# Forget gates of all heads made in three steps between Strassen pairs, with one PSUM bank for each product

## The chip, the cores and the metric

The kernel runs on one core of a Trainium2 chip. A core has a matrix engine (TensorE, PE in the rows) with its weight load (PEld), an elementwise engine (VectorE, DVE), an activation engine (ScalarE, ACT), a general one (GpSimd, POOL), and SyncE (SP), which here only issues transfers. Each has its own queue and works it in order; they wait for one another by semaphores. The metric is the time of one execution in microseconds (us), the median of several runs.

## The reference

One decoder block on 512 tokens of width 1024, in float32. The change touches the combined input projection and the gated linear attention (GLA, 4 heads, key width 128, value width 256, chunks of 64 tokens):

```
h = rms_norm(x);  proj = h @ w_in          # q, k, v, r, low-rank a, NSA q/k/v, gates
log_a = log_sigmoid(a_lr @ w_alpha2 + b_alpha) / 16
b = cumsum(log_a) inside each chunk;  b_last = b at the chunk's end
qe, ke, kd = q*exp(b), k*exp(-b), k*exp(b_last - b)
o = causal(qe @ ke^T) @ v + qe @ state;  state = exp(b_last)*state + kd^T @ v
o = rms_norm(o) * silu(r)
x = x + rms_norm((sig(gA)*(o @ w_gla) + sig(gB)*(nsa @ w_nsa)) @ w_out)
x = x + rms_norm(swiglu(rms_norm(x)))
```

## The kernel before

Every float32 operand of the large products is held as a high and a low part, and a product is three matmuls (high by high, high by low, low by high). The program is one stream of instructions for each engine; Python loops write it, and a scheduler fixes the order in each queue when the kernel is built, by its own estimate of when operands are there. `tc.issue_after(x)` puts what is made under it behind instruction x in its engine's order.

**Stages.** Up to 42.5 us of the span, part of the input projection is made token-major (`tok_chunk`). Then come eleven *pairs* of output tiles (loop at L542): each pair is one 2x2 Strassen step on two tiles of 128 columns of `w_in`, with 7 products of 12 matmuls of 256 columns (`in_unit`, L384 to L423). Pairs 0 to 3 are q and k of the four GLA heads (`gq`, `gk`), 4 to 7 the eight tiles of r (`rr`), 8 the selected and window keys (`kst`), 9 and 10 the NSA queries (`qst`). They end at 163.84 us. Then comes linear attention (`gla_prep`, `gla_attn`, `gla_turn`, `gla_state`, `gla_out`, `gla_end` for each head), put by the table `when` (L759) between steps of other matmuls: 16 steps that make the values of heads 2 and 3 (`values_step`) and then eighths of dense products. After 250 us follow sparse attention, projections and the feed-forward part.

**A pair.** The first tile g is loaded into one of three `wraw` buffers, the second tile u into one of two `urw` (L328, issued two pairs ahead by SP; pair 0 has them the other way round). VectorE makes four sums of them (`in_sums`, L355 to L358: s1, s2 in one `ssum` buffer, s3, s4 in the other). Sums and raw tiles are split: ScalarE casts the high part (L221, L336), and the low part is a subtraction on VectorE (L222) or, for raw tiles, a negated copy on ScalarE (L337) and an accumulating transfer on GpSimd's queue (L338). The parts live in five slots used in turn (`s0`, `s1`, `s2`, and two of `whi`/`wlo`); those of a22 in `uu`. In this order the products are: a11 into r1, s2 into r2, s3 into rb, s1 into ra, a22 added to rb, s4 added to ra, a12 added to r1. After the first, ScalarE copies r1 to `us` (L403); VectorE adds r2 to it (`us`, L400), then makes `us` + rb before a22 may be added to rb, and so on; the last part is a copy on ScalarE (L415) and a scaling (L418, L421); r tiles get a Silu on ScalarE (L423).

**Banks.** PSUM has eight banks, two for each of the tags sc, mm, acc and tp. A pair uses both banks of one tag (r1 and rb in halves of the first, r2 and ra in halves of the second), and the tag changes from pair to pair.

**Gates.** `gate_logs` (L427) makes the forget gates of two heads: load the second-layer weights (GpSimd), clear and fill `w3` (VectorE), four transposes of the low-rank columns of `tokb`, copies (`aT`), for each head one gate product (L445) with an Abs on ScalarE (L446) and a min on VectorE (L447), then Exp and Ln on both heads (L449, L450), each function in its own table that ScalarE loads first (ACT_TABLE_LOAD), and for each head a subtraction and a scan along the tokens (L452, L453). It runs in pair 6 for heads 0 and 1 (`early_gates`, tiles `ge`) and in linear attention for heads 2 and 3 (`late_gates`, tiles `gl`, at step 5 of `when`).

**A head of linear attention.** `gla_prep` makes five exponentials on ScalarE (L598 to L604: `e1`, two parts of `e2`, `dd`, and the small `el`; `el`, `dd` and most products have two buffers), `dec` (L606) and four products on VectorE, and four on GpSimd (L616, L620 to L622) that use `el` and `dd`. `gla_attn` has four matmuls and a masked copy into `at` on VectorE (L634), `gla_turn` three transposes and a copy `gkut` on ScalarE, `gla_state` three products (L650), each in its own tp bank (there are two), read by ScalarE (L652) or VectorE, `gla_out` seven products (L666, L668), four squares (L669) and four scaled copies on ScalarE, `gla_end` eight transposes (L682).

## Time and profile before

| | before |
|---|---|
| median of three runs | 872.01 us (871.56, 872.01, 1165.77) |
| the profiled execution | 871.92 us, of which the span of the trace is 870.1 us |
| mean granted clock of TensorE | 0.988 of full speed |
| busy: TensorE / VectorE / ScalarE / GpSimd | 840.0 / 652.2 / 534.8 / 155.7 us |
| stage 0 to 42.5 us | TensorE busy 41.45 of 42.50 us |
| pairs, 42.5 to 163.84 us | TensorE busy 114.90 of 121.34 us, clock 0.97 |
| linear attention, 163.84 to 250 us | TensorE busy 75.70 of 86.16 us, clock 0.96 |
| the rest, 250 to 870 us | TensorE busy 607.92 of 620.00 us, clock 0.99 |

The span runs from the first to the last instruction in the trace; the time of an execution has 1.8 us more. A timeline row gives the start, the length, engine, line, operation, output<-inputs, shapes and count, and in brackets how long the engine had been idle before it and which instruction ended that. Matmuls overlap their neighbours, so their lengths add up to more than the time between starts. Tile names stand without buffer numbers. The clock is given as a share of the full 2.4 GHz.

### The profile page before, as it was taken

The page shows a single profiled execution, that of the slowest core. Times are in us where ns is not written, and L with a number is a line of the kernel's source. Part 1 is how long each engine was busy: PE and PEld are TensorE (multiplying, and loading weights), DVE is VectorE, ACT ScalarE, POOL GpSimd, SP SyncE. Part 2 cuts the span into 40 slices and gives each one's busy share as a digit, 9 for nine tenths or more (in the row PEclk, how much of TensorE's full clock was granted, in tenths as well). Part 3 has the DMA queues.
Part 4 walks back from the last instruction along what each step waited for, and adds up shares of the span by engine and source line. Part 5 has one row for each costly group of instructions (what it writes and reads, how often), then busy time and mean ns, then how long its engine had stood idle before and what let it go on. Part 6 is the DMA issues. An engine that isn't in the chain of part 4 may idle for free.

```text
span 870.1 us, 14830 instructions
## 1 busy us (share of the span) xinstructions
PE 840.0 (97%) x5632; PEld 765.3 (88%) x5632; DVE 652.2 (75%) x1219; ACT 534.8 (61%) x945; POOL 155.7 (18%) x186
## 2 busy tenths in 40 slices
PE   9999989978999999999999999999999999999995
PEld 8999979957788788888887999899999999889995
DVE  7888768755465888887767468998778779838886
ACT  6765666456453788888744576866666557535441
POOL 0121112213030001000000354111111110001353
PEclk9999989989999999999999999999999999999998
DMA  7588755211142434544316849679877872225222
GB/s 258 153 222 189 156 135 125 74 50 47 34 155 66 121 85 114 118 112 107 86 49 218 277 137 250 138 194 226 185 174 189 192 173 76 93 88 169 87 97 98
DMA packets 43463, 119.99 MB, mean 138 GB/s; under 512 B 5772, under 2 KB 11164, under 8 KB 43264
## 3 DMA queue, kind: packets, MB, share of 16 engines
q1 hardware_dynamic: 30576, 82.49, 29.7%
q0 software_dynamic: 12096, 36.01, 22.6%
q8 instruction: 44, 0.72, 0.3%
q10 hardware_dynamic: 720, 0.54, 0.2%
q14 instruction: 27, 0.22, 0.1%
HBM read 104.34 MB, written 4.19 MB: 125 GB/s over the span
## 4 chain that ended last, share of the span: by engine, by line
PE 81%; ACT 5%; DVE 3%; POOL 2%; issue 1%; DMA 1%; DVEq 0%; ACTq 0%; POOLq 0%
PE ps_mm L204 6%; PE ps_mm L206 6%; PE ps_mm L205 6%; PE ps_mm L1425 6%; PE ps_sc L1425 6%; PE ps_tp L1425 6%; PE ps_acc L1425 5%; PE ps_sc L1717 4%; PE ps_mm L396 3%; PE ps_acc L396 3%; PE ps_sc L396 3%; PE ps_acc L1717 2%; PE ps_mm L1717 2%; PE ps_tp L396 2%; PE ps_tp L1026 2%
## 5 line engine op out<-in xcount | busy, mean ns | idle before, releaser
L79 ACT CAST whi<-wraw 128x1024 fp32r<-128x1024 f32 (+3 forms) x58 | 56.2, 970 | 58.9 <-issue 18.0
L204 PE MATMUL ps_mm<-hT_hi,whi 128*128 128x512 f32 x168 | 69.3, 412 | 0.0
L205 PE MATMUL ps_mm<-hT_lo,whi 128*128 128x512 f32 x168 | 66.8, 398 | 0.0
L206 PE MATMUL ps_mm<-hT_hi,wlo 128*128 128x512 f32 x168 | 66.8, 398 | 0.0
L85 DVE TENSOR_TENSOR wlo<-wraw,whi 128x1024 fp32r<-128x1024 f32 (+3 forms) x43 | 46.7, 1087 | 20.6 <-ACT whi L79 20.5
L83 POOL DMA_DIRECT2D wlo<-wraw x15 | 13.0, 864 | 159.9 <-ACT wlo L82 159.9
L986 ACT ACTIVATE p<-p,mx 128x512 f32<-128x512 f32 (+1 forms) x64 | 35.9, 561 | 8.5 <-DVE mx L984 7.8
L222 DVE TENSOR_TENSOR pl<-ps_tp,ph 128x512 fp32r<-128x512 f32 (+1 forms) x64 | 31.0, 489 | 13.4 <-ACT ph L221 12.8
L206 PEld LDWEIGHTS ps_mm<-hT_hi,wlo 128*128 128x128 f32 x168 | 31.6, 188 | 7.6 <-DVE wlo L85 0.3
L204 PEld LDWEIGHTS ps_mm<-hT_hi,whi 128*128 128x128 f32 x168 | 31.7, 188 | 6.4
L205 PEld LDWEIGHTS ps_mm<-hT_lo,whi 128*128 128x128 f32 x168 | 31.7, 189 | 5.3
L984 DVE CUSTOM_DVE_ANT_0 p<-ps_sc,causal 128x512 f32<-128x512 f32 (+1 forms) x64 | 30.2, 485 | 6.0 <-PE ps_sc L977 5.8
L1324 POOL DMA_DIRECT2D w_uu<-in_w_up x19 | 16.4, 865 | 87.2 <-ACT w_uu L1322 20.4
L221 ACT CAST ph<-ps_tp 128x512 fp32r<-128x512 f32 (+1 forms) x64 | 26.3, 415 | 4.6 <-PE ps_tp L1026 3.8
L1026 PE MATMUL ps_tp<-ident,p 128*128 128x128 f32 x160 | 27.7, 273 | 0.4 <-ACT pc L920 0.3
L1026 PEld LDWEIGHTS ps_tp<-ident,p 128*128 128x128 f32 x160 | 20.6, 140 | 7.9 <-ACT pc L920 0.7
L204 PE MATMUL ps_mm<-gla_hi,whi 128*128 128x512 f32 x64 | 26.1, 408 | 0.0
L1340 ACT CAST w_d1h<-s 128x1024 fp32r<-128x1024 f32 x13 | 13.6, 1050 | 20.2 <-issue 12.5
L206 PE MATMUL ps_mm<-gla_hi,wlo 128*128 128x512 f32 x64 | 25.2, 394 | 0.0
L205 PE MATMUL ps_mm<-gla_lo,whi 128*128 128x512 f32 x64 | 25.2, 393 | 0.0
L1340 ACT CAST w_hl<-s 128x1024 fp32r<-128x1024 f32 x12 | 12.6, 1047 | 16.6 <-issue 14.6
L1340 ACT CAST w_d0h<-s 128x1024 fp32r<-128x1024 f32 x13 | 13.6, 1048 | 13.5 <-issue 12.4
(1153 smaller groups left out, 3373.0 us busy)
## 6 DMA issues: line engine op xcount, KB each, us to landing
wraw<-in_w_t SPq DMA_DIRECT2D x29, 512.0 KB, 3.8
wraw<-in_w_gate SPq DMA_DIRECT2D x21, 512.0 KB, 5.8
rw<-in_w_up SPq DMA_DIRECT2D x19, 512.0 KB, 4.2
wlo<-wraw POOLq DMA_DIRECT2D x15, 512.0 KB, 4.5
...
```

What stands on the lines that cost most here:

```text
L79: self.cast = self.nc.scalar.copy(hi[:, :cols], raw[:, :cols])
L85: self.nc.vector.tensor_tensor(out=lo[:, :cols], in0=raw[:, :cols], in1=hi[:, :cols].bitcast(F32), op=OP.subtract)
L204: pe.matmul(ps[:, t], wh[:, c], xh(k)[:, t], start=(k == 0), stop=False)
L205: pe.matmul(ps[:, t], wh[:, c], xl(k)[:, t], start=False, stop=False)
L206: marks.append(pe.matmul(ps[:, t], wl[:, c], xh(k)[:, t], start=False, stop=(k == ktot - 1)))
L222: dve.tensor_tensor(out=lo, in0=src, in1=hi.bitcast(F32), op=OP.subtract)
L396: pe.matmul(o, w[:, c], x_of(b, q, low), start=(first and q == 0 and i == 0), stop=(q == 3 and i == 2), skip_group_check=True)
L986: act.activation(out=o, in_=o, func=AF.Exp, scale=-1.0, bias=mx[:, i:i + 1], accum_out=z[:, i:i + 1])
L1026: pe.transpose(tp[:, i * 128:(i + 1) * 128], p[:, OFF[i] + k * 128:OFF[i] + (k + 1) * 128], ident)
L1340: act.copy(hi, t)
L1425: pe.matmul(o, w[:, c], x[q], start=(first and q == 0 and i == 0), stop=(q == 3 and i == 2), skip_group_check=True)
L1717: pe.matmul(o, w[:, c], x[q], start=(first and q == 0 and i == 0), stop=(q == KH - 1 and i == 2), skip_group_check=True)
```

## The change

- **Banks.** Each product of a pair has a bank of its own: r1, r2, rb, ra lie in four banks, (sc, sc, mm, mm) in even pairs and (acc, acc, tp, tp) in odd ones. There is one `us` tile in place of two.
- **Sums.** s3 and s4 are written over the raw tile u in `urw`; there is one `ssum` buffer. The freed room holds the gates of all four heads (`lam01`, `lam23`).
- **Gates.** `gate_logs` is cut into `gates_low` (weights, transposes, `aT`; in pair 3), `gates_in` (gate products, Abs, min; heads 0, 1 in pair 4, heads 2, 3 in pair 5), `gates_logs` (four Exp, four Ln, in pair 5's turn of the loop) and `gates_sums` (subtractions and scans; heads 0, 1 in pair 6, heads 2, 3 in pair 7). `late_gates` is gone.
- **Silu.** All eight are made together after pair 7 (`silu_r`), followed by one small Exp that loads that table. Table loads on ScalarE fall from 9 to 5 in the program.
- **Pairs.** The NSA queries come before the selected and window keys.
- **Linear attention.** The table `when` is spread anew, and `gla_state` puts its first two products in one bank.
- Two small ones: `ones` is one column that is broadcast, and in pair 0 the split of a22 is made before the sums.

The core of the diff:

```diff
+    lam23 = tokv.tile([128, 2, S], F32, name="lam23")
+    spare = tokv.tile([128, 2, S], F32, tag="lam01", name="spare")
...
-    ssum = [s1.tile([128, 1024], F32, name="ssum%d" % i) for i in range(2)]
+    ssum = [s1.tile([128, 1024], F32, name="ssum"), spare.rearrange("p a t -> p (a t)")]
...
-    pairs += [(T_KV + 2, T_KV + 3), (T_NQ, T_NQ + 1), (T_NQ + 2, T_NQ + 3)]
+    pairs += [(T_NQ, T_NQ + 1), (T_NQ + 2, T_NQ + 3), (T_KV + 2, T_KV + 3)]
...
-        g, u, (a, b) = graw[j], uraw[j], ssum
+        g, u, a = graw[j], uraw[j], ssum[0]
...
-        dve.tensor_tensor(out=b[:, lo], in0=g[:, lo], in1=u[:, lo], op=OP.subtract)
-        dve.tensor_tensor(out=b[:, hi], in0=g[:, hi], in1=a[:, hi], op=OP.subtract)
+        dve.tensor_tensor(out=u[:, lo], in0=g[:, lo], in1=u[:, lo], op=OP.subtract)
+        dve.tensor_tensor(out=u[:, hi], in0=g[:, hi], in1=a[:, hi], op=OP.subtract)
...
-        split(hi, lo, ssum[names[0] == "s3"])
+        split(hi, lo, uraw[j] if names[0] == "s3" else ssum[0])
...
+    def in_banks(j):
+        return (("sc", "mm"), ("acc", "tp"))[j % 2]
+
     def in_unit(j):
-        tag = ("sc", "mm", "acc", "tp")[j % 4]
         d1, d2 = [in_dst(n) for n in pairs[j]]
-        p1, p2 = bank(tag), bank(tag)
-        r1, rb, r2, ra = p1[:, 0:256], p1[:, 256:512], p2[:, 0:256], p2[:, 256:512]
-        us = us2[j % 2]
+        r1, r2, rb, ra = [bank(tag)[:, 0:256] for tag in in_banks(j) for _ in range(2)]
+        us = us2[0]
...
-        product(rb, "s3", "t3", False)
+        product(rb, "s3", "t3", True)
         add(us[:, 1, :], rb, us[:, 0, :])
-        product(ra, "s1", "t1", False)
+        product(ra, "s1", "t1", True)
...
-            if n >= T_R:
-                act.activation(out=t, in_=t, func=AF.Silu)
+
+    def silu_r():
+        with tc.issue_after(gst["act"].ins):
+            for t in [rr[i ^ 1] for i in range(8)]:
+                last = act.activation(out=t, in_=t, func=AF.Silu)
+        with tc.issue_after(last.ins):
+            act.activation(out=warm, in_=mhalf[:, 0:1], func=AF.Exp)
...
+    def gates_low(tag):
+        w_a2, keep = place("ksts", [16, 512], F32), place("kstw", [128, 8, 64], F32)
+        aT, w3 = place("qst0", [80, S], F32R), place("qst1", [80, S], F32R)
...
+        gst.update(a=aT, w=w3, keep=keep, low=[])
+        lam01 = tokv.tile([128, 2, S], F32, tag="lam01", name="lam01")
+        for h in range(HG):
+            lams[h] = (lam01, lam23)[h // 2][:, h % 2, :]
...
+    def gates_in(hs, tag):
+        for h in hs:
             ps = bank(tag)
-            pe.matmul(ps, w3[:, h * 128:(h + 1) * 128], aT, start=True, stop=True)
-            act.activation(out=lam[:, i], in_=ps, func=AF.Abs, bias=b_alpha[:, h:h + 1])
-            dve.tensor_scalar(out=lows[i], in0=ps, scalar1=b_alpha[:, h:h + 1], scalar2=0.0,
-                              op0=OP.add, op1=OP.min)
-        act.activation(out=lam, in_=lam, func=AF.Exp, scale=-1.0)
-        act.activation(out=lam, in_=lam, func=AF.Ln, bias=1.0)
-        for i, h in enumerate(hs):
-            dve.tensor_tensor(out=lam[:, i], in0=lows[i], in1=lam[:, i], op=OP.subtract)
-            dve.tensor_tensor_scan(out=lam[:, i], data0=keep.rearrange("p c t -> p (c t)"), data1=lam[:, i],
+            pe.matmul(ps, gst["w"][:, h * 128:(h + 1) * 128], gst["a"], start=True, stop=True)
+            gst["act"] = act.activation(out=lams[h], in_=ps, func=AF.Abs, bias=b_alpha[:, h:h + 1])
+            low = us2[1] if h == 3 else place(("qst2", "qst3", "ksts")[h], [128, S], F32)
+            dve.tensor_scalar(out=low, in0=ps, scalar1=b_alpha[:, h:h + 1], scalar2=0.0, op0=OP.add, op1=OP.min)
+            gst["low"].append(low)
...
+    def gates_logs():
+        for f, kw in ((AF.Exp, dict(scale=-1.0)), (AF.Ln, dict(bias=1.0))):
+            with tc.issue_after(gst["act"].ins):
+                for h in range(HG):
+                    last = act.activation(out=lams[h], in_=lams[h], func=f, **kw)
+            gst["act"] = last
...
+    def gates_sums(hs):
+        for h in hs:
+            dve.tensor_tensor(out=lams[h], in0=gst["low"][h], in1=lams[h], op=OP.subtract)
+            dve.tensor_tensor_scan(out=lams[h], data0=gst["keep"].rearrange("p c t -> p (c t)"), data1=lams[h],
...
-        if j == 6:
-            in_raw_forms(j + 2)
...
+        with tc.issue_after(after.ins), tc.issue_after(queued["pool"].ins):
+            if j == 3:
+                gates_low("tp")
+            elif j == 4:
+                gates_in((0, 1), "mm")
+            elif j == 5:
+                gates_in((2, 3), "tp")
...
-        if j == 6:
-            with tc.issue_after(after.ins), tc.issue_after(queued["pool"].ins):
-                early_gates()
-        if j + 2 < NP and j != 6:
...
+        if j + 2 < NP:
             in_raw_forms(j + 2)
+        if j == 5:
+            gates_logs()
+        elif j in (6, 7):
+            with tc.issue_after(after.ins):
+                gates_sums(((0, 1), (2, 3))[j - 6])
+        if j == 7:
+            silu_r()
...
+        pss = [bank("tp"), bank("tp")]
         for n in range(3):
-            ps = bank("tp")
-            pe.matmul(ps[:, 0:256], kut[:, n, :], value(h, n), start=True, stop=True)
+            ps = pss[n // 2][:, n % 2 * 256:n % 2 * 256 + 256]
+            pe.matmul(ps, kut[:, n, :], value(h, n), start=True, stop=True)
...
-    for at, f, h in ((0, gla_prep, 1), (3, gla_attn, 0), (5, gla_turn, 0), (6, gla_state, 0), (6, gla_attn, 1),
+    for at, f, h in ((0, gla_prep, 1), (3, gla_attn, 0), (5, gla_turn, 0), (6, gla_state, 0), (7, gla_attn, 1),
                      (8, gla_out, 0), (8, gla_turn, 1), (9, gla_prep, 2), (10, gla_state, 1), (12, gla_end, 0),
-                     (12, gla_out, 1), (13, gla_prep, 3), (15, gla_attn, 2), (16, gla_end, 1), (17, gla_turn, 2),
-                     (20, gla_attn, 3), (21, gla_state, 2), (22, gla_turn, 3), (24, gla_out, 2), (27, gla_state, 3),
-                     (31, gla_end, 2), (31, gla_out, 3), (39, gla_end, 3)):
+                     (13, gla_out, 1), (14, gla_prep, 3), (15, gla_attn, 2), (17, gla_end, 1), (18, gla_turn, 2),
+                     (20, gla_attn, 3), (22, gla_state, 2), (23, gla_turn, 3), (25, gla_out, 2), (28, gla_state, 3),
+                     (32, gla_end, 2), (33, gla_out, 3), (41, gla_end, 3)):
...
-    when.setdefault(5, []).append(gates23)
```

What follows shows how instructions stand in the queues before and after; names are the program's, a number behind a name tells buffers apart. The changed file has its own line numbers: L400, L403, L415 and L221 of before are L404, L407, L419 and L222 there, L446 and L449/L450 are L467 and L476, L598 to L604 are L620 to L626.

On ScalarE, before, the logs of heads 0 and 1 (`lam_1305`) stand behind the copy `us` of pair 7's first product (L403) and the cast of a sum, with a table load ahead of each function:

```order
L403 COPY us_425<-ps_tp 128x256
L221 CAST whi<-ssum_164 128x1024
L446 ACTIVATE lam_1305<-ps_mm,vecs 128x512 x2
L449 ACT_TABLE_LOAD
L449 ACTIVATE lam_1305<-lam_1305 128x1024
L221 CAST s0h<-ssum_165 128x1024
L450 ACT_TABLE_LOAD
L450 ACTIVATE lam_1305<-lam_1305 128x1024
```

After the change the same place is at the end of pair 5 (L419 copies its last product); `lam_978` are heads 0 and 1, `lam_159` heads 2 and 3, and the Abs of heads 0 and 1 were made a pair earlier:

```order
L419 COPY r_140<-ps_acc 128x256
L467 ACTIVATE lam_159<-ps_tp,vecs 128x512 x2
L476 ACTIVATE lam_978<-lam_978 128x512 x2
L476 ACTIVATE lam_159<-lam_159 128x512 x2
L476 ACT_TABLE_LOAD
L476 ACTIVATE lam_978<-lam_978 128x512 x2
L476 ACTIVATE lam_159<-lam_159 128x512 x2
L407 COPY us<-ps_sc 128x256
L222 CAST s0h<-ssum 128x1024
L222 CAST whi<-urw_165 128x1024
```

What moved: two Abs, four Exp, a table load and four Ln now stand ahead of the copy of pair 6's first product (L407), where half of that work stood behind such a copy before.

On ScalarE at the start of linear attention, before, the exponentials of heads 0 and 1 (both from `lam_1305`) are followed by a weight cast (L79) and by the copy `gkut` of head 0 (L642):

```order
L598 ACTIVATE e_1798<-lam_1305 128x512
L601 ACTIVATE e_1799<-dd 128x4x64
L602 ACTIVATE e_1799<-lam_1305 128x4x64
L603 ACTIVATE dd<-dd 128x512
L604 ACTIVATE el<-lam_1305 128x8
L598 ACTIVATE e_1838<-lam_1305 128x512
L601 ACTIVATE e_1839<-dd 128x4x64
L602 ACTIVATE e_1839<-lam_1305 128x4x64
L603 ACTIVATE dd<-dd 128x512
L604 ACTIVATE el<-lam_1305 128x8
L79 CAST whi<-wraw 128x1024
L642 COPY gkut<-ps_tp 128x384
```

After, from the `el` of head 1 (its first row) to `gkut` (L664):

```order
L626 ACTIVATE el<-lam_978 128x8
L624 ACTIVATE e_1882<-lam_978 128x4x64
L626 ACTIVATE el<-lam_159 128x8
L623 ACTIVATE e_1882<-dd 128x4x64
L625 ACTIVATE dd<-dd 128x512
L620 ACTIVATE e_2027<-lam_159 128x512
L624 ACTIVATE e_2028<-lam_159 128x4x64
L626 ACTIVATE el<-lam_159 128x8
L79 CAST whi<-wraw 128x1024
L623 ACTIVATE e_2028<-dd 128x4x64
L625 ACTIVATE dd<-dd 128x512
L664 COPY gkut<-ps_tp 128x384
```

What moved: the small `el` of heads 2 and 3 (from `lam_159`) and the exponentials of head 2 now stand ahead of the cast and of `gkut`; `el` still has two buffers.

On VectorE in pair 2, before, a sum of s3, s4 (L357, L358) is written into the second `ssum` buffer, `ssum_165`, from which L222 makes the low part:

```order
L400 TENSOR_TENSOR gq_149<-ps_acc,us_424 128x256
L222 TENSOR_TENSOR s0l<-ssum_165,s0h 128x1024
L400 TENSOR_TENSOR gq_149<-ps_acc,us_424 128x256
L357 TENSOR_TENSOR ssum_165<-wraw,urw_162 128x512
L400 TENSOR_TENSOR gk_153<-ps_acc,us_424 128x256
L418 SCALAR_TENSOR_TENSOR gq_149<-gq_149,rb_x 128x512
L358 TENSOR_TENSOR ssum_165<-wraw,ssum_164 128x512
L421 TENSOR_TENSOR gk_153<-gk_153,rb_x 128x512
```

After, they are written over u itself (`urw_164`, L360, L361), and the low part of the pair before is made from `urw_165`:

```order
L360 TENSOR_TENSOR urw_164<-wraw,urw_164 128x512
L404 TENSOR_TENSOR gq_149<-ps_mm,us 128x256
L223 TENSOR_TENSOR s0l<-urw_165,s0h 128x1024
L404 TENSOR_TENSOR gq_149<-ps_mm,us 128x256
L361 TENSOR_TENSOR urw_164<-wraw,ssum 128x512
L404 TENSOR_TENSOR gk_153<-ps_mm,us 128x256
L422 SCALAR_TENSOR_TENSOR gq_149<-gq_149,rb_x 128x512
L425 TENSOR_TENSOR gk_153<-gk_153,rb_x 128x512
```

What moved: L360 stands one addition earlier than L357 did, and a `urw` buffer is now read by the split L223, so the load that refills it comes behind that split.

## Rows read from the trace of the kernel before

**Rows 1.** Part 1 of the profile's page: busy time, share of the span and instructions of each engine.

```profile
PE 840.0 (97%) x5632; PEld 765.3 (88%) x5632; DVE 652.2 (75%) x1219; ACT 534.8 (61%) x945; POOL 155.7 (18%) x186
```

**Rows 2.** Windows view, of pair 3 and of linear attention. Columns: stretch, its length, busy time and instructions of TensorE, its weight loads, VectorE, ScalarE, GpSimd, granted clock, share of the DMA engines, GB/s.

```profile
74.22:84.17 9.95, 9.95 (x86) 9.95 (x85) 8.04 (x14) 5.62 (x9) 1.73 (x2) 1.00 0.79 184
...
163.84:250.00 86.16, 75.70 (x354) 60.78 (x353) 49.18 (x81) 49.50 (x112) 26.74 (x38) 0.96 0.20 61
```

**Rows 3.** Timeline of TensorE: ten of its instructions that waited, from 47 to 232 us.

```profile
47.07 0.39 PE L396 MATMUL ps_sc<-tfh,s2h 128*128 128x256 f32 x1 [1.30 <-ACT us L403]
...
97.80 0.38 PE L396 MATMUL ps_mm<-tfh,s2h 128*128 128x256 f32 x1 [0.41 <-ACT us L403]
...
118.93 0.39 PE L396 MATMUL ps_tp<-tfh,whi 128*128 128x256 f32 x1 [0.28 <-ACT us L403]
...
124.07 1.22 PE L445 MATMUL ps_mm<-ge,ge 80*128 80x512 f32 x2 [3.69 <-DVE ge L442]
...
138.32 0.39 PE L396 MATMUL ps_sc<-tfh,whi 128*128 128x256 f32 x1 [0.75 <-DVE us L400]
...
181.14 1.22 PE L445 MATMUL ps_tp<-gl,gl 80*128 80x512 f32 x2 [4.81 <-DVE gl L442]
...
193.86 0.70 PE L666 MATMUL ps_sc<-tok,at 128*128 128x256 f32 x2 [1.70 <-ACT go L669]
...
199.77 0.70 PE L650 MATMUL ps_tp<-tok,gkut 128*128 128x256 f32 x2 [1.16 <-ACT gs L652]
...
215.27 0.66 PE L682 MATMUL ps_tp<-ident,go 128*128 128x128 f32 x4 [1.40 <-DVE at L634]
...
231.73 0.70 PE L650 MATMUL ps_tp<-tok,gkut 128*128 128x256 f32 x2 [1.08 <-ACT gs L652]
```

**Rows 4.** Windows view, columns as in rows 2: stretches around four of these waits.

```profile
44.00:50.00 6.00, 4.70 (x39) 4.49 (x39) 4.94 (x8) 3.97 (x8) 1.73 (x2) 1.00 0.71 197
124.00:129.00 5.00, 4.93 (x21) 4.74 (x22) 4.59 (x9) 4.07 (x5) 0.00 (x0) 0.50 0.21 62
181.00:187.00 6.00, 5.86 (x15) 4.62 (x15) 2.72 (x4) 4.01 (x6) 0.00 (x0) 0.50 0.07 13
192.00:196.00 4.00, 2.30 (x11) 1.82 (x11) 3.48 (x9) 3.96 (x13) 0.04 (x1) 1.00 0.00 0
```

**Rows 5.** Timeline of ScalarE: a table load and the Silu behind it (pair 5), the two Abs of heads 0 and 1, and the first exponentials of linear attention.

```profile
95.04 1.28 ACT L423 ACT_TABLE_LOAD   x1
96.33 1.15 ACT L423 ACTIVATE r<-r 128x512 f32<-128x512 f32 x2
...
124.90 1.26 ACT L446 ACTIVATE lam<-ps_mm,vecs 128x512 f32<-128x512 f32 x2 [5.08 <-PE ps_mm L445]
...
165.72 0.63 ACT L598 ACTIVATE e<-lam 128x512 f32<-128x512 f32 x1
166.26 0.40 ACT L601 ACTIVATE e<-dd 128x256 f32<-128x256 f32 x1
```

**Rows 6.** Timeline of VectorE: the split of the sums s3, s4 of pair 3 (71.11), the first sum of pair 5 (77.61) and the addition in pair 3 that the fifth product waits for (78.94), and the subtraction and scan of heads 0 and 1.

```profile
71.11 1.22 DVE L222 TENSOR_TENSOR s0l<-ssum,s0h 128x1024 fp32r<-128x1024 f32 x1 [0.58 <-ACT s0h L221]
...
77.61 0.68 DVE L355 TENSOR_TENSOR ssum<-urw 128x512 f32<-128x512 f32 x1
...
78.94 0.42 DVE L400 TENSOR_TENSOR us<-ps_tp,us 128x256 f32<-128x256 f32 x1
...
132.88 1.28 DVE L452 TENSOR_TENSOR lam<-ge,lam 128x512 f32<-128x512 f32 x2
134.08 2.33 DVE L453 TENSOR_TENSOR_SCAN lam<-ge,lam 128x512 f32<-128x512 f32 x2
```

**Rows 7.** DMA view: issue to landing of a load of `urw`, first of the one issued at 73.3 us, then of the one issued at 47.0 us.

```profile
DMA to landing us min/median/max: 4.5/4.5/4.5
...
DMA to landing us min/median/max: 8.7/8.7/8.7
```

**Rows 8.** Timelines of GpSimd and of VectorE: the first and the last of the products that GpSimd makes for heads 0 and 1, and `dec` of head 0 and of a later head.

```profile
167.57 0.98 POOL L620 TENSOR_TENSOR gkx<-gk,dd 128x256 f32<-128x256 f32 x1 [19.86 <-ACT dd L603]
...
173.13 2.04 POOL L622 TENSOR_TENSOR gku<-gkx,el 128x256 f32<-128x256 f32 x1
...
167.87 0.70 DVE L606 TENSOR_TENSOR dec<-el 128x4 f32<-128x4 f32 x1
...
194.62 0.16 DVE L606 TENSOR_TENSOR dec<-el 128x4 f32<-128x4 f32 x1 [0.28 <-ACT el L604]
```

**Rows 9.** Timelines of ScalarE, VectorE and TensorE at the start of linear attention: the last large exponential of head 0, a weight cast, the masked copy of head 0, the split behind the cast; then the first value matmul, the transposes of the late gates and the matmul behind them.

```profile
166.87 0.62 ACT L603 ACTIVATE dd<-dd 128x512 f32<-128x512 f32 x1
...
169.30 1.05 ACT L79 CAST whi<-wraw 128x1024 fp32r<-128x1024 f32 x1
...
172.92 0.67 DVE L634 COPY_PREDICATED at<-triu,ps_tp 128x512 f32<-128x512 uint8 x1
173.49 1.20 DVE L85 TENSOR_TENSOR wlo<-wraw,whi 128x1024 fp32r<-128x1024 f32 x1
...
163.84 0.39 PE L302 MATMUL ps_mm<-whi,hT_hi 128*128 128x512 f32 x1
...
173.64 0.60 PE L439 MATMUL ps_tp<-ident,tokb 128*16 128x128 f32 x4 [0.17 <-DVE at L634]
174.00 0.48 PE L302 MATMUL ps_acc<-whi,hT_hi 128*128 128x512 f32 x1
```

More of the change, by code (lines that the diff above doesn't have):

```diff
@@ L126, in hybrid_block_kernel @@
     make_identity(nc, ident)
-    ones = base.tile([128, 128], F32, name="ones")
-    dve.memset(ones, 1.0)
+    one = base.tile([128, 1], F32, name="ones")
+    ones = one.to_broadcast([128, 128])
+    dve.memset(one, 1.0)
     mhalf = base.tile([128, 16], F32, name="mhalf")
@@ L511, in forms_room @@
         a, b = [[s2.tile([128, 1024], F32R, name="s%d%s" % (i, x)) for x in "hl"] for i in (1, 2)]
-        us2.extend(s2.tile([128, 2, 256], F32, name="us%d" % i) for i in range(2))
+        us2.append(s2.tile([128, 2, 256], F32, name="us"))
+        us2.append(s2.tile([128, S], F32, name="low"))
         slots[0] = a
```

34 lines of the change are left out of this document (9 added, 25 removed).

## Prediction

> **What bounds the kernel now.** I read four views, in this order. The busy line of the page [rows 1] puts TensorE at 97% of the span: work on other engines counts only where TensorE waits for it, or where a wait lowers its clock. The windows [rows 2] show where there is anything to win. A pair of input tiles in the steady part (pair 3) takes 9.95 us with TensorE never idle, VectorE busy for 8.04 us of it and ScalarE for 5.62 us. The linear attention, from 163.84 to 250 us, has TensorE idle for about 10.5 us of 86.16. The timeline of TensorE [rows 3] names the waits. Inside pairs there are four short ones (1.30, 0.41, 0.28, 0.75 us), where a product waits for a bank that another engine still reads; the two gate products wait 3.69 and 4.81 us for VectorE; linear attention adds 1.70, 1.16, 1.40 and 1.08 us. The clock windows [rows 4] show what follows the two long waits: the granted clock is 0.50 (1.2 GHz) in 124 to 129 and 181 to 187 us, while after the waits of 1.30 and 1.70 us it is 1.00 (2.4 GHz). Half clock fills these stretches from each restart (124.07 to 129, 181.14 to 187) and costs half of its length; with a little beyond their ends I take 5.2 and 6.0 us, so 2.6 and 3.0 us.
>
> **What the change removes.** Both long waits come from the gates being made in one piece. VectorE reaches the first use of the second-layer weights before their load has landed, and TensorE stands behind it. After the change the load is issued in pair 3, its first user comes after pair 3, the gate products follow pairs 4 and 5, and there is no second set. That takes out 3.69 + 4.81 = 8.50 us of waits, 5.6 us of half clock, and one set of four transposes (173.64 to 174.00, where the next product starts: 0.36 us [rows 9]). A bank for each product lets the third and fourth product start without a reader to wait for; the fifth still has to wait for the read of the third, but that read has another product's time. Of the four bank waits I strike all: 2.74 us. In linear attention the four waits, 5.34 us, all change place; I strike them and price the new ones below. Removed: 8.50 + 5.6 + 0.36 + 2.74 + 5.34 = 22.5 us.
>
> **What it adds, place by place.** One product is 9.95 / 7 = 1.42 us, one matmul of 256 columns 9.95 / 84 = 0.118 us and one of 512 about 0.23.
>
> *Pair 6, ScalarE.* The new order puts two Abs, four Exp, a table load and four Ln between the end of pair 5 and the copy of pair 6's first product (`us`). Before, the first Abs starts 0.83 us after its gate product (124.07 to 124.90), two Abs take 1.26 us, an Exp on 128x512 has a pitch of 0.54 us (165.72 to 166.26), and a load takes 1.28 us [rows 3, 5]. With E the end of pair 5: 0.83 + 1.26 + 2.16 + 1.28 + 2.16 = E + 7.7, and the copy ends at E + 8.1. TensorE has two gate products (0.61 us at full clock, half of the 1.22 shown), four products and two matmuls of the next pair, to E + 6.5. It waits 1.5 us; bounds 0.8 (copies and casts overlap) and 2.5. The Trainium skill, in "ScalarE: Activation LUTs", section "What ACT_TABLE_LOAD costs", puts a switch of tables at about 2.66 us, a drain included. The trace has 1.28 us and the next activation 0.01 us behind it [rows 5], so no such drain is seen; by the page the wait would be 2.9 us and the total below 858.9.
>
> *Pairs 4, 7 and 8, VectorE.* It has 9.95 - 8.04 = 1.9 us to spare in a pair. The sums of two heads cost 1.28 + 2.33 = 3.6 us [rows 6] and now fall into pair 7 and again into pair 8, ahead of the two `us` additions that the fifth product waits for: 1.7 us too much in pair 7. About 0.4 us of it disappears in the wait of pair 6, and I take 1.3 us. In pair 8 the sums stand partly behind the first addition; with pair 4, which gets the low-rank work, and pair 9, I take 0.4 us. Bounds for the two together 0.3 and 4.
>
> *Loads of the second input tile.* The sums now overwrite it, so its buffer is free only when the split of the third product's form (`s0l`, 71.11 + 1.22 = 72.33, which is 1.9 us before pair 3 starts at 74.22) has read it; before, it was free a pair earlier than it was needed. The load for two pairs on must land before VectorE's first sum, at 77.61 [rows 6]. With 4.5 us to landing [rows 7] it lands at 76.9: 0.7 us spare. The fifth product, at 74.22 + 4 x 1.42 = 79.90, needs the second addition, done at 78.94 + 0.42 = 79.36, so VectorE may be 0.54 us later still. So a landing may take 5.28 us from the split (72.33 to 77.61), or 5.8 before TensorE feels it. Early on one took 8.7 us [rows 7]: there the load for pair 3 would be 3.4 us late and TensorE wait 2.9 us in pair 1. Between 4.5 and 8.7 I take the middle, 6.6 us: 0.8 us of wait in pair 1, bounds 0 and 2.9.
>
> *Linear attention, head 0.* ScalarE's new order has the small decay exponentials of heads 2 and 3 (`el`) ahead of a weight cast and of the copy `gkut`. `el` has two buffers, so these rows wait until GpSimd has used those of heads 0 and 1. With E the end of the last pair: no table load, exponentials from E + 0.6 to the end of `dd` at E + 2.4 (before 165.72 to 167.49, the same 1.8 us). GpSimd's eight products take up to 0.98 us each and the last up to 2.04 [rows 8], so they end between E + 2.4 + 8 x 0.98 = E + 10.2 and E + 11.3. VectorE is slow beside them: a 128x4 product takes 0.70 us there and 0.16 us elsewhere [rows 8]. Then cast (1.05), VectorE's split of it (1.20) and the masked copy of head 0 (0.67) [rows 9]: E + 13.1 to E + 14.2. That copy frees the bank for the state products. TensorE reaches them after 42 value matmuls and two small groups, by the pace of before (163.84 to 173.64 - 0.17 = 173.47, plus six at 0.23 us) at E + 11.0. It waits 2.1 to 3.2 us; I take 2.4, near the lower end, since a product or two may run beside the exponentials. Lower bound 0.5, if the products and casts run beside one another; upper 3.2.
>
> *Linear attention, later heads.* The state products of one head now lie in two banks and the squares come in an order in which a full bank is never waited for at once; head 1's output still stands behind two casts on ScalarE. I take 0.7 us there and 1.0 us elsewhere, against 5.34 before; bounds 0.5 and 4.
>
> Moves at no cost: the Silu activations wait until pair 6 to 9, hidden by ScalarE's 4.3 us of spare time a pair (without that, half a microsecond each); four of nine table loads go, all off the path except the one before the first exponential, which is counted above in the start at E + 0.6. After 250 us the order is the same but for a few neighbours, and TensorE is never idle for long, so what is won is kept.
>
> **The sum.** Added: 1.5 + 1.3 + 0.4 + 0.8 + 2.4 + 1.7 = 8.1 us. 22.5 - 8.1 = 14.4 us less. The profiled execution took 871.92 us (span 870.1 and 1.8 around it), 0.1 from the median of 872.01: 857.5 us.
>
> **Rivals.**
> *The new waits stay hidden.* All my added terms but the last rest on engines running at their rates of before with nothing overlapping; if the orders slide into each other, only about 1.7 us is added: 871.9 - 22.5 + 1.7 = 851 us. For it speaks that VectorE and ScalarE both have spare time in every pair; against it that the orders are fixed, and an engine works in its order. 18%.
> *The clock falls again.* The wait of 2.4 us lies between 1.70, which left the clock alone, and 3.69, which did not. If it falls there, 3.0 us go; if the two waits of pairs 6 and 7 together cause one, 2.6 more; and with the waits near their upper bounds another 2 to 3: 861 to 866 us. 20%.
> *The loads of the second tile come late in every pair.* If landings were 8.7 us not only early on, the load would land at 72.33 + 8.7 = 81.0 and not 76.9, so TensorE would wait the 2.9 us worked out above in each of eight pairs, 23 us: 881 us, and with a clock that falls each time (2.6 us) 902. From a landing of about 7.6 us on (1.8 us a pair) the change loses all that it wins. Against it: the landing of 4.5 us was measured in a steady pair, beside the other loads of that pair. 5%. The Trainium skill's "TensorE: Matmul & The Clock Gate", section "HAM oscillation", describes just this, a wait for data that returns at every tile and lets the clock fall each time; no run shown here has a wait in every pair, and single ones of 1.30 and 1.70 us left it at 2.4 GHz.
>
> **How the numbers follow.** The forecast, 57%, covers 852 to 863. Two per cent, about what a measurement of this kernel can tell from no change, is below 854.6 or above 889.5. Below: the first rival and a tail of 7% of the forecast, 25%. Above: the last rival with the clock falling, 3%. The rest is 72%. For 8 in 10, the range goes from 849.5 (the first rival, with a microsecond of bank waits less) to 866 (the second).
>
> **What would show it.** Right: the gate products (L445 before) start without a wait; the granted clock is 1.00 from 100 to 250 us; five table loads; waits of 1 to 2 us before the last product of pair 6 (ScalarE's `us`) and the fifth of pair 7 (VectorE's `us`); the first state product waits about 2.4 us for VectorE's masked copy. Wrong: a first sum on VectorE that waits for the `urw` transfer in pair after pair, a slice below 1.00, or no wait at the state products.

## The result, and the profile after

| | before | after |
|---|---|---|
| median | 871.56 us (871.18 to 872.01; one run of 1165.77 left out) | 859.69 us (858.82 to 860.12) |
| ratio, 95% interval | | 0.9862 (0.9843 to 0.9882) |
| profiled execution, its span | 871.92, 870.1 us | 859.46, 857.7 us |
| pairs: start, end, length | 42.50, 163.84, 121.34 us | 43.04, 159.45, 116.41 us |

The change takes 11.9 us off the time, 1.4%; 14.4 were forecast, and 859.7 lies in the range of 849.5 to 866. The span is 12.4 us shorter. TensorE is busy 3.7 us less than in [rows 1], about what less half clock gives (it counts as busy then); the other 8.7 us were waiting. Part 1 of the page of the changed kernel:

```profile
PE 836.3 (98%) x5628; PEld 763.4 (89%) x5628; DVE 649.3 (76%) x1213; ACT 529.4 (62%) x944; POOL 153.2 (18%) x183
```

Timeline of TensorE after the change, all its waits of 0.3 us and more from 30 to 240 us, and its gate products (L466, the L445 of before):

```profile
53.92 0.38 PE L400 MATMUL ps_acc<-hT_hi,wlo 128*128 128x256 f32 x1 [0.37 <-DMA wlo<-in_w_t]
60.51 0.39 PE L400 MATMUL ps_tp<-tfh,uu 128*128 128x256 f32 x1 [0.87 <-DVE us L404]
...
95.32 0.63 PE L466 MATMUL ps_mm<-g_qst,g_qst 80*128 80x512 f32 x2
105.78 0.64 PE L466 MATMUL ps_tp<-g_qst,g_qst 80*128 80x512 f32 x2
...
113.78 0.39 PE L400 MATMUL ps_sc<-hT_hi,whi 128*128 128x256 f32 x1 [1.44 <-ACT us L407]
124.81 0.39 PE L400 MATMUL ps_tp<-tfh,uu 128*128 128x256 f32 x1 [0.78 <-DVE us L404]
172.52 1.10 PE L673 MATMUL ps_tp<-tok,gkut 128*128 128x256 f32 x4 [1.88 <-DVE at L656]
188.15 0.70 PE L673 MATMUL ps_tp<-tok,gkut 128*128 128x256 f32 x2 [1.27 <-ACT gs L675]
205.28 0.52 PE L663 MATMUL ps_tp<-ident,gku 128*128 128x128 f32 x3 [1.52 <-DVE sr L708]
219.78 0.70 PE L673 MATMUL ps_tp<-tok,gkut 128*128 128x256 f32 x2 [0.61 <-ACT gs L675]
```

Against [rows 3]: the gate products start without a wait, and eight waits add up to 8.74 us (8.1 were forecast). Six of them are new. The two for `gs` (1.27 and 0.61 us) stand where 1.16 and 1.08 us stood before: at the last state product of heads 1 and 3, until ScalarE has copied the first state. The clock, in the windows of this execution and then of a second one of the same kernel (run e0_after_again); the clock is the third number from the end:

```profile
170.00:180.00 10.00, 8.12 (x33) 6.39 (x32) 5.17 (x8) 3.33 (x7) 2.31 (x3) 0.83 0.22 58
```

```profile
170.00:180.00 10.00, 9.39 (x47) 7.91 (x48) 4.81 (x11) 3.90 (x12) 2.08 (x4) 1.00 0.34 107
```

In the first the clock falls to 1.2 GHz behind the wait of 1.88 us, which costs (1 - 0.83) x 10 = 1.7 us; in the second the same wait stands at 170.61 us and the clock stays. That execution took 856.04 us and lacks the two early waits too: 3.4 us less, of which 1.7 + 1.24 = 2.9 are these two.

### The profile page after: what moved, and what is told of

Its sections match the earlier page's. It is cut to its first block, busy times and chain, and to the rows that moved or that the text cites. A ratio compares the mean times of both kernels' runs of the same rounds, so it can differ in the third digit from the quotient of the medians.

```text
span 857.7 us, 14807 instructions
## 1 busy us (share of the span) xinstructions
PE 836.3 (98%) x5628; PEld 763.4 (89%) x5628; DVE 649.3 (76%) x1213; ACT 529.4 (62%) x944; POOL 153.2 (18%) x183
## 4 chain that ended last, share of the span: by engine, by line
PE 82%; ACT 8%; DVE 4%; issue 3%; POOL 2%; DMA 1%; DVEq 0%; POOLq 0%; ACTq 0%
PE ps_mm L205 6%; PE ps_mm L1442 6%; PE ps_mm L207 6%; PE ps_sc L1442 6%; PE ps_mm L206 6%; PE ps_tp L1442 6%; PE ps_acc L1442 5%; PE ps_sc L1734 4%; PE ps_tp L400 3%; PE ps_mm L400 2%; PE ps_acc L1734 2%; PE ps_mm L1734 2%; PE ps_tp L1043 2%; PE ps_sc L400 1%; PE ps_acc L400 1%
## 5 line engine op out<-in xcount | busy, mean ns | idle before, releaser
L79 ACT CAST whi<-wraw 128x1024 fp32r<-128x1024 f32 (+3 forms) x58 | 56.2, 969 | 62.6 <-issue 17.8
L223 DVE TENSOR_TENSOR pl<-ps_tp,ph 128x512 fp32r<-128x512 f32 (+1 forms) x64 | 31.0, 489 | 13.1 <-ACT ph L222 12.5
L1341 POOL DMA_DIRECT2D w_uu<-in_w_up x19 | 16.5, 867 | 86.9 <-ACT w_uu L1339 20.4
L222 ACT CAST ph<-ps_tp 128x512 fp32r<-128x512 f32 (+1 forms) x64 | 26.4, 416 | 4.2 <-PE ps_tp L1043 3.6
L1357 ACT CAST w_d0h<-s 128x1024 fp32r<-128x1024 f32 x13 | 13.6, 1048 | 13.5 <-issue 12.4
```

Of the source, the lines that this page charges most:

```text
L79: self.cast = self.nc.scalar.copy(hi[:, :cols], raw[:, :cols])
L223: dve.tensor_tensor(out=lo, in0=src, in1=hi.bitcast(F32), op=OP.subtract)
L1357: act.copy(hi, t)
```

## The experiments

Edits are shown in short form. Each run is given as us below the kernel before, as run beside it on the same chip (its median was 870.85, 871.28, 871.48 and 870.72 us in the four sets).

**The changed kernel again.** No edit.

> The changed kernel itself beside the same runs of the kernel before as the next three: 0.985 to 0.988 of it, and in the trace the same waits of 1.44, 0.78 and 1.88 us, with half clock after the last alone.

Measured: 859.43 us, ratio 0.9869 (0.985 to 0.9888), 11.9 us less. The clock did not fall in its profiled execution, against what was expected (above).

### What holds the state products of head 0

```diff
-        el = gt.tile([128, 8], F32, tag="el", bufs=2, name="el")
+        el = gt.tile([128, 8], F32, tag="el", bufs=4, name="el")
```

> The changed kernel with four buffers for the small decay exponentials (el) in place of two, nothing else. In the changed kernel's trace the first state product waits 1.88 us for VectorE's masked copy and the clock is 0.50 from about 173.9 to 177.3 us, some 3.4 us, which costs 1.7. Theory A (ScalarE standing at el behind GpSimd is what makes the masked copy late): both go, 859.7 - 1.9 - 1.7 = about 856. Theory B (VectorE's two subtractions of 2.24 us and the weight split stand ahead of the masked copy anyway): the copy ends at 167.58 + 2.24 + 1.23 + 0.73 = 171.8 and not 172.37, so the wait only shrinks to about 1.2 to 1.3 us: 859.1 if the clock falls all the same, 857.4 if it does not.

Measured: 857.95 us, ratio 0.9844 (0.9831 to 0.9858), 12.9 us less; theory B, with a clock that stays, though the wait is 1.56 us and not 1.2 to 1.3. The interval overlaps that of the changed kernel (0.985 to 0.9888): the trace tells the theories apart, the time alone would not. First ScalarE of the changed kernel at the two rows in question, and VectorE and GpSimd there; then VectorE and TensorE of this run:

```profile
165.35 0.21 ACT L626 ACTIVATE el<-lam 128x8 f32<-128x8 f32 x1 [1.98 <-POOL gku L644]
...
169.31 0.22 ACT L626 ACTIVATE el<-lam 128x8 f32<-128x8 f32 x1 [1.20 <-POOL gku L644]
169.43 1.03 ACT L79 CAST whi<-wraw 128x1024 fp32r<-128x1024 f32 x1
...
167.58 2.24 DVE L619 TENSOR_TENSOR dd<-lam 128x512 f32<-128x512 f32 x2
170.50 1.23 DVE L85 TENSOR_TENSOR wlo<-wraw,whi 128x1024 fp32r<-128x1024 f32 x1 [0.68 <-ACT whi L79]
171.64 0.73 DVE L656 COPY_PREDICATED at<-triu,ps_tp 128x512 f32<-128x512 uint8 x1
...
168.22 1.06 POOL L644 TENSOR_TENSOR gku<-gkx,el 128x256 f32<-128x256 f32 x1
```

```profile
169.04 1.09 DVE L619 TENSOR_TENSOR dd<-lam 128x512 f32<-128x512 f32 x1 [0.64 <-POOL gku L643]
...
172.61 1.10 PE L673 MATMUL ps_tp<-tok,gkut 128*128 128x256 f32 x4 [1.56 <-DVE at L656]
```

ScalarE did stand at `el` for 1.98 and 1.20 us, but without that the masked copy comes only 0.3 us sooner: VectorE's two subtractions L619 for heads 2 and 3 stand ahead of it, and the second now waits for GpSimd itself, by `dd`, which has two buffers like `el`. So both rows were moved:

```diff
+        with tc.issue_after(held[h - 2].ins), tc.issue_after(turned[h - 2].ins):  # h > 1
+            gla_prep_in(h)          # held: masked copy (L656), turned: copy gkut (L664)
```

> The changed kernel with the preparation of heads 2 and 3 held back on VectorE behind the masked copy of heads 0 and 1, and on ScalarE behind the copy gkut of heads 0 and 1; el keeps two buffers. Theories A and B of the first run both expect that the wait of 1.88 us at the state products goes, and with it the half clock: 859.7 - 1.9 - 1.7 = 856.1, a little more if the preparations held back make a later head wait. Theory C (the clock falls because this stretch is made of small products, not because of the wait): the wait goes but the clock is still 0.50 for some 3 us: 857.8.

Measured: 855.59 us, ratio 0.9821 (0.9806 to 0.9836), 15.3 us less. The wait is gone, the clock is 1.00 in every window from 42 to 242 us, and no later head waits longer:

```profile
170.00:180.00 10.00, 10.00 (x52) 8.32 (x51) 5.15 (x11) 5.42 (x17) 2.70 (x4) 1.00 0.24 87
```

One such window would not settle theory C, since e0_after_again kept its clock with the wait. But the four later runs with this edit (e8, e9, e13, e14) are at 1.00 there too, so it has nothing for it: without the wait this stretch kept 2.4 GHz in five executions of five.

### What holds pairs 6 to 9

```diff
-        if j == 5: gates_logs()                       # four Exp, load, four Ln
+        if j == 5: gates_logs(Exp)
+        if j == 6: gates_logs(Ln), behind the copy us of pair 6
-        elif j in (6, 7): gates_sums(...)
+        elif j in (7, 8): gates_sums(...)
```

> The changed kernel with the four Ln and their table load put behind the copy us of pair 6, and the sums of the gates one pair later (pairs 7 and 8). Theory A (the wait of 1.44 us in pair 6 is ScalarE's row of logs and nothing else): it goes, and the sums cost what they cost now: 858.2. Theory B (ScalarE has too little spare time there whatever the order, since a table load, four Ln and the eight Silu follow one another): the wait appears in pair 7 at ScalarE's copy or at a cast: 859.2 to 860.5.

Measured: 860.12 us, ratio 0.986 (0.984 to 0.988), 10.7 us less, so no gain. Timelines of VectorE and of TensorE in this run:

```profile
110.52 0.42 DVE L404 TENSOR_TENSOR us<-ps_sc,us 128x256 f32<-128x256 f32 x1 [1.49 <-ACT us L407]
114.87 1.23 DVE L223 TENSOR_TENSOR wlo<-urw,whi 128x1024 fp32r<-128x1024 f32 x1 [1.25 <-ACT whi L222]
125.30 1.23 DVE L223 TENSOR_TENSOR s0l<-urw,s0h 128x1024 fp32r<-128x1024 f32 x1 [1.08 <-ACT s0h L222]
...
123.34 0.39 PE L400 MATMUL ps_tp<-tfh,uu 128*128 128x256 f32 x1 [1.00 <-DVE us L404]
135.61 0.39 PE L400 MATMUL ps_mm<-tfh,uu 128*128 128x256 f32 x1 [1.17 <-DVE us L404]
145.70 0.39 PE L400 MATMUL ps_tp<-tfh,uu 128*128 128x256 f32 x1 [0.68 <-DVE us L404]
```

The wait of 1.44 us is gone and 2.85 us stand in pairs 7 to 9, where 0.78 stood. Given back, as theory B says. All three name VectorE, and not ScalarE, which theory B named; but VectorE had itself stood 1.49, 1.25 and 1.08 us behind ScalarE's copy and casts, so this run does not part the two engines. The logs were therefore spread forward, the sums left where they are, and the preparations held back as above:

```diff
+        if j == 4: gates_logs(Exp, heads 0, 1)
+        if j == 5: gates_logs(Exp, heads 2, 3); gates_logs(Ln, heads 0, 1)
+        if j == 6: gates_logs(Ln, heads 2, 3), behind the copy us of pair 6
```

> The changed kernel with the preparations held back as in the run e6_prep_held, and the logs spread: Exp of heads 0 and 1 in pair 4, Exp of heads 2 and 3 and the table load and Ln of heads 0 and 1 at the end of pair 5, Ln of heads 2 and 3 behind the copy us of pair 6. The sums stay in pairs 6 and 7. Theory A (the wait in pair 6 is the length of ScalarE's row, and it can be moved in front of earlier copies that have time): the 1.44 us go, and nothing else changes: 1.4 us below e6_prep_held's ratio, 0.9805 of the kernel before. Theory B (VectorE was held by the same wait, and what TensorE saves in pair 6 it waits in pair 7 for the sums): 0.5 us or less below it, with a wait in pair 7 of 1.5 us and more.

Measured: 856.54 us, ratio 0.9828 (0.9813 to 0.9843): no gain over e6_prep_held, theory B in its sum. TensorE waits 0.55, 0.69 and 1.15 us for VectorE in pairs 6, 7 and 8 and 0.84 us for a low part, 3.23 us against 1.44 + 0.78. Windows of the changed kernel show what stands behind it; the third busy time is VectorE's, and the row under them is VectorE's too:

```profile
120.00:130.00 10.00, 9.22 (x77) 9.01 (x77) 9.79 (x16) 8.29 (x14) 1.76 (x2) 1.00 0.72 148
130.00:140.00 10.00, 9.93 (x82) 9.56 (x81) 9.96 (x17) 7.31 (x12) 2.63 (x3) 1.00 0.80 160
140.00:150.00 10.00, 10.00 (x87) 10.00 (x86) 9.71 (x16) 5.27 (x8) 2.37 (x4) 1.00 0.75 160
150.00:160.00 10.00, 10.00 (x84) 9.91 (x83) 5.71 (x10) 1.58 (x5) 0.00 (x0) 1.00 0.37 110
...
113.76 0.43 DVE L404 TENSOR_TENSOR us<-ps_sc,us 128x256 f32<-128x256 f32 x1 [4.99 <-ACT us L407]
```

VectorE is full for 30 us. Part of that may be work held back, since just before it stands idle for 4.99 us behind ScalarE's copy. Relief on ScalarE shortens this idle time (2.92 us in this run) but not the work, and VectorE is busy here for 10.00 us of each 10 from 120 to 140 us. Less work for VectorE:

```diff
-   Abs (ScalarE), min (VectorE), Exp, Ln, subtract and scan (VectorE)
+   Exp(-x - b) straight from the bank, Ln(1 + .), scan;  T = -1/16 in gla_prep
```

> The changed kernel with the preparations held back as in the run e6_prep_held, and the gates in a shorter form: ln(1 + exp(-x)) straight from the product with its sign turned in the exponents of linear attention, so no Abs, no min and no subtraction. It takes some 1.3 us from ScalarE's row in front of the copy us of pair 6 (2.19 / 2 for two Exp, the Exp in the place of the Abs) and 4 x 0.70 + 4 x 0.65 = 5.4 us from VectorE in pairs 4 to 8. It holds for gate inputs above about -88, the form before for any. Theory A (in pairs 6 to 9 VectorE is the bound: it is busy for 9.7 to 10 us of every 10 from 120 to 150 us, and relief on ScalarE alone was given back there): the waits of 1.44 and 0.78 us both go and none takes their place: 2.2 us below e6_prep_held, ratio about 0.9795. Theory B (another bound stands behind it, a transfer or ScalarE's Silu): no more than 1 us below e6_prep_held, with waits in pairs 7 to 9 that name a transfer or ScalarE.

Measured: 856.54 us, ratio 0.9828 (0.9815 to 0.9841): no gain over e6_prep_held, as theory B says, but the waits left do not name what it named. The 1.44 us are gone, but waits of 0.59, 0.76 and 0.91 us for VectorE's `us` stand in pairs 6 to 8. The two scans alone (2.33 us) and the steady 8.04 us [rows 2] make 10.4 us in a pair of 9.95, and VectorE is still busy for 9.97 us from 120 to 130 us. In pair 6 ScalarE stands behind the wait: VectorE is idle for 4.23 us there until ScalarE's copy. From 150 us on VectorE has room:

```diff
-        elif j in (6, 7): gates_sums(((0, 1), (2, 3))[j - 6])
+        elif j in (8, 9): gates_sums(((0, 1), (2, 3))[j - 8])
```

> The kernel of e9_less_vector_work with the scans of the gates two pairs later, in pairs 8 and 9. VectorE makes the sums of the pairs ahead of time, so it has 8.0 us of work in a pair up to pair 8 and is busy for 6 us of 10 from there on. Theory A (VectorE's amount of work in pairs 7 and 8, 8.0 + 2.3 of 9.95 us, makes the waits of 0.76 and 0.91 us left in that run): both go, nothing comes in pairs 8 to 10: 1.7 us below e9_less_vector_work, ratio about 0.981; the 0.59 us in pair 6 stay. Theory B (not the amount but the order of the additions on VectorE, or a transfer): a wait of 0.5 us and more stays in pair 7 or 8, or comes in pair 9: within 0.7 us of it.

Measured: 854.19 us, ratio 0.9809 (0.9796 to 0.9822), 16.5 us less; theory A. No wait is left in pairs 7 to 10; the 0.59 us in pair 6 stay, as expected. Its windows:

```profile
120.00:130.00 10.00, 10.00 (x86) 9.91 (x85) 7.92 (x14) 8.74 (x14) 1.73 (x2) 1.00 0.92 206
130.00:140.00 10.00, 10.00 (x85) 9.81 (x84) 9.71 (x15) 7.40 (x12) 1.73 (x2) 1.00 0.66 143
140.00:150.00 10.00, 10.00 (x87) 10.00 (x86) 8.29 (x12) 4.03 (x6) 1.50 (x3) 1.00 0.51 112
```

By the medians this is the fastest version tried. Its interval lies below those of both kernels and overlaps that of e6_prep_held (0.9806 to 0.9836).

### The parts of the change by themselves

```diff
-        tag = ("sc", "mm", "acc", "tp")[j % 4]; p1, p2 = bank(tag), bank(tag)     # kernel before
+        r1, r2, rb, ra = [bank(tag)[:, 0:256] for tag in tags for _ in range(2)]
```

> The kernel before with one part of the change alone: a bank of its own for each of the four results of a pair. Theory A (the four bank waits of rows 3 are a matter of banks): 1.30, 0.41, 0.28 and most of 0.75 us go and nothing comes: 2.0 to 2.7 us below the kernel before. Theory B (the fifth product must wait for the same two additions anyway, and what TensorE does not wait at the third it waits at the fifth): 0.3 to 1.0 us below it.

Measured: 868.57 us, ratio 0.9964 (0.9952 to 0.9977), 2.7 us less: theory A. Three of the four waits are gone, 0.75 became 0.43, and pair 0 waits 0.77 us for a low part instead of 1.30 for the bank. The long waits stay, 4.23 and 4.82 us. So the short waits in pairs fall by 1.5 us net and the first long one grows by 0.5. In the profiled execution the half clock behind it is shorter too, with a granted clock of 0.83 from 120 to 130 us where the kernel before has 0.66, so the 2.7 us are not the bank waits alone:

```profile
120.00:130.00 10.00, 8.40 (x57) 8.21 (x58) 8.31 (x14) 7.51 (x9) 0.00 (x0) 0.83 0.27 75
```

The early load by itself:

```diff
+    w_a2 = tokv.tile([16, 512], F32, name="w_a2")      # kernel before, at the start
+    pool.dma_start(w_a2, I["w_alpha2"])
-        pool.dma_start(w_a2, I["w_alpha2"])            # in gate_logs, twice
```

> The kernel before with nothing changed but the load of the second-layer weights: one tile, loaded at the start, read by both sets of gates. Theory A (the late landing of this load makes both long waits): the gate products of heads 0 and 1 come without a wait (3.69 and 2.6 us of half clock gone), those of heads 2 and 3 with one of about 0.6 us (VectorE is free at 174.69 and needs 2.3 us; TensorE idles from 176.33), so 4.2 and 3.0 us gone there: 13.5 us below the kernel before, more than the whole change takes. Theory B (the gates' chain through VectorE, TensorE and ScalarE is too long in one piece, whenever the weights are there): waits of 2 us and more stay at both places, and at least one of the two stretches of half clock: 3 to 8 us below it.

Measured: 865.19 us, ratio 0.9927 (0.9914 to 0.9941), 6.1 us less, in theory B's range but not by its cause. Timeline of TensorE, then the landing of s1l (DMA view, its load was issued at 116.6 us):

```profile
119.76 0.64 PE L446 MATMUL ps_mm<-ge,ge 80*128 80x512 f32 x2
...
125.50 0.58 PE L398 MATMUL ps_sc<-hT_hi,s1l 128*128 128x256 f32 x1 [2.83 <-DMA s1l<-in_w_t]
...
177.01 0.74 PE L446 MATMUL ps_tp<-gl,gl 80*128 80x512 f32 x2 [1.53 <-DVE gl L443]
...
188.21 0.70 PE L667 MATMUL ps_sc<-tok,at 128*128 128x256 f32 x2 [1.88 <-ACT go L670]
```

```profile
DMA to landing us min/median/max: 8.9/8.9/8.9
```

Of the waits of the gate products the first is gone and the second falls from 4.81 to 1.53 us (theory A: 0.6), so the load is what made them. VectorE's rows of the kernel before show it waiting for that load:

```profile
121.72 0.42 DVE L434 CAST ge<-ge 16x512 fp32r<-16x512 f32 x1 [4.02 <-DMA ge<-in_w_alpha]
...
178.80 0.41 DVE L434 CAST gl<-gl 16x512 fp32r<-16x512 f32 x1 [4.11 <-DMA gl<-in_w_alpha]
```

But TensorE now reaches the next pair's low part before it has landed, and waits 2.83 us with half clock behind it. In the kernel before the same load also took 8.9 us, under the wait of 3.69. And half clock follows a wait of 1.88 us in linear attention.

Both edits together:

> The kernel before with both small parts: the second-layer weights loaded at the start (e5_early_load, 6.1 us) and a bank for each result (e3_banks_only, 2.7 us), all else as before. Theory A (the parts are separate): 8.8 us below the kernel before, ratio 0.990. Theory B (the bank saved is taken by the low parts that land late, the wait of 2.83 us in e5_early_load, since TensorE now reaches them sooner): 6 to 7 us below it, ratio 0.992 to 0.993.

Measured: 858.81 us, ratio 0.9851 (0.9836 to 0.9866), 12.7 us less: more than the two apart (8.8), outside both theories, and as much as the whole change. With banks of its own TensorE's order no longer has pair 8's first product ahead of pair 7's fifth, so it comes to s1l at 126.33 us, when it has landed (issued at 115.9, 9.0 us); the gate products wait 0.22 and 1.51 us, and the clock is 1.00 from 42 to 242 us.

```profile
126.33 0.28 PE L397 MATMUL ps_sc<-hT_hi,s1l 128*128 128x256 f32 x1
```

Some of the gain over the sum may be chance: linear attention has a wait of 1.87 us here that left the clock alone, and one of 1.88 us in e5_early_load that did not.

The reverse, the changed kernel with the shared banks of before:

```diff
-        r1, r2, rb, ra = [bank(tag)[:, 0:256] for tag in in_banks(j) for _ in range(2)]
+        tag = ("sc", "mm", "acc", "tp")[j % 4]; p1, p2 = bank(tag), bank(tag)
```

> The changed kernel with the banks of before: r1 and rb share a bank, r2 and ra share one, the tag changes from pair to pair; the gates take the banks of tags that the pair does not use. Theory A (the four bank waits of before, 2.74 us, come from sharing): they come back in whole or for the greater part, 861.7 to 862.5. Theory B (the waits of before came from what else ScalarE and VectorE had to do just then, and sharing alone costs little): within 0.7 us of the changed kernel, 859.0 to 860.4.

Measured: 864.8 us, ratio 0.9925 (0.9912 to 0.9938): 6.0 us less than the kernel before where the changed kernel has 11.9, outside both theories. Timeline of TensorE:

```profile
47.20 0.39 PE L402 MATMUL ps_sc<-tfh,s2h 128*128 128x256 f32 x1 [1.10 <-ACT us L409]
114.33 0.58 PE L402 MATMUL ps_tp<-hT_hi,s2l 128*128 128x256 f32 x1 [4.94 <-DMA s2l<-in_w_t]
129.25 0.39 PE L402 MATMUL ps_tp<-tfh,s0h 128*128 128x256 f32 x1 [0.89 <-DVE us L406]
139.34 0.38 PE L402 MATMUL ps_sc<-tfh,whi 128*128 128x256 f32 x1 [0.32 <-DVE us L406]
```

Three waits for a shared bank came back, 1.10 us at a third product and 0.89 and 0.32 at fourth products (pairs 0, 7 and 8): 2.31 us of the 2.74, as theory A says, though not all at the places of before. The 4.94 us are the low part of pair 7, which TensorE's order, with shared banks, uses behind the second product of pair 6. They are why the time fits neither theory, and they show the other thing that banks do: they set TensorE's order.

**The first state copied by VectorE**, on top of e9_less_vector_work:

```diff
-                act.copy(ss[:, 0, :], ps)
+                dve.tensor_copy(ss[:, 0, :], ps)
```

> The kernel of e9_less_vector_work with one more edit: the first state of each head is copied from its bank by VectorE and not by ScalarE. Theory A (the waits of 1.27 and 0.60 us before a state product come from ScalarE's row of squares and scaled copies, and VectorE is free there): both go, 1.9 us below e9_less_vector_work. Theory B (the copy comes late because the bank is written late): within 0.5 us of it.

Measured: 856.07 us, ratio 0.9823 (0.9808 to 0.9838), 0.5 us below e9_less_vector_work by the medians: theory B's number. The wait of 0.60 us is gone, that of 1.27 is 1.13 and names VectorE now. ScalarE, VectorE and TensorE there:

```profile
181.96 1.57 ACT L702 ACTIVATE go<-ps_sc,grs 128x256 f32<-128x256 f32 x4 [1.20 <-POOL grs L237]
...
184.24 0.42 DVE L646 TENSOR_TENSOR gkx<-gk,e 128x256 f32<-128x256 f32 x1 [3.79 <-ACT e L629]
184.59 0.42 DVE L680 COPY gs<-ps_tp 128x256 f32<-128x256 f32 x1
...
182.20 1.03 PE L678 MATMUL ps_tp<-tok,gkut 128*128 128x256 f32 x4
185.06 0.70 PE L678 MATMUL ps_tp<-tok,gkut 128*128 128x256 f32 x2 [1.13 <-DVE gs L680]
```

Theory B's cause does not hold: the bank is written by 183.23 us and the copy starts at 184.59. On VectorE the copy stands behind a product `gkx` that waits 3.79 us for an exponential of ScalarE, and that one stands behind the four scaled copies `go`. So ScalarE's row, theory A's cause, holds the copy on either engine.

## Why the prediction was right, and where it was off

*What the change removes.* Right in amount: 8.50 us at the gate products, their half clock and the bank waits are gone. The cause was half right. "The gates being made in one piece" is not what made the long waits: with the load early and the gates in one piece the first goes and 1.5 of 4.81 us is left of the second (e5_early_load, e10_load_and_banks). The load, which the prediction names as well, is the cause of all but that. The bank waits were put at 2.74 us; banks alone gave 2.7. That they agree is in part luck: the waits in pairs fell by only 1.0 us there, net, and the half clock was shorter in the profiled execution (e3_banks_only).

*Pair 6.* Forecast 1.5 us, measured 1.44, by ScalarE's copy `us`, as worked out. The table load takes 1.28 us here too. By the price in the Trainium skill's "ScalarE: Activation LUTs", section "What ACT_TABLE_LOAD costs", the estimate would have been 2.9; the measured wait decides for 1.28.

*Pairs 4, 7, 8, 9.* Forecast 1.7 us, measured 0.78, all in pair 7. The reason, that the sums exceed VectorE's spare time, is borne out by e14, where the waits went when the scans moved. What was missed is that it holds for pairs 6 to 9 together, and that VectorE stands idle for 4.99 us behind ScalarE's row in pair 6 before it is full: the wait of pair 6 could not be taken out by itself (e2, e8, e9).

*Loads of the second tile.* Forecast 0.8 us in pair 1, measured 0.87 (with 0.37 in pair 0 for a low part). The load issued at 51.9 us landed after 6.7 us, the middle value taken; VectorE's first sum waited for it:

```profile
58.70 0.69 DVE L358 TENSOR_TENSOR ssum<-urw 128x512 f32<-128x512 f32 x1 [1.38 <-DMA urw<-in_w_t]
```

From 62 us on the landings are 3.7 to 5.1 us and no sum waits: the third rival did not come.

*Head 0.* Forecast 2.4 us, measured 1.88. GpSimd's eight products ended at 169.28, E + 9.8 (E + 10.2 to 11.3). The masked copy was late as worked out, but `el` was only one of two things ahead of it (e1_el4, e6_prep_held); VectorE's subtractions for heads 2 and 3 were the other.

*Later heads.* Forecast 1.7 us, measured 1.27 + 1.52 + 0.61 = 3.40. This is the term that was mis-sized most: it was set by guess where the others were worked out from rows. One of the three waits (1.52 us) is for VectorE behind a weight split. The other two are for the first state's copy and stood in [rows 3] already: the prediction struck them because a head's products now lie in two banks, but the product that shares the first state's bank still waits until that is copied, 1.27 for 1.16 us and 0.61 for 1.08. What delays the copy is ScalarE's row of scaled copies (e13_state_on_vector).

*The clock.* The second rival, 20%, came true in the profiled execution (1.7 us for the 3.0 forecast) and not in the second one.

*The sum.* Removed 22.5; added 1.44 + 0.78 + 1.24 + 1.88 + 3.40 = 8.74, and 1.7 of half clock; the pairs begin 0.54 us later, which no edit explains (42.61 in e14, 43.30 in e1). 22.5 - 8.74 - 1.7 - 0.54 = 11.5; measured between the two profiled executions 871.92 - 859.46 = 12.5. The missing microsecond lies mostly in linear attention. From its start to the same product of sparse attention (298.96 us before, 286.62 after) 7.95 us went. The terms give 4.81 + 3.0 + 0.36 + 5.34 removed, 0.61 for the gate products that moved into the pairs, and 1.88 + 3.40 + 1.7 against it: 7.1. What the rest is stays open.
